# Accumulators of the last convolution tile in PSUM, a running sum issued behind a K eviction, and two V tiles ahead of the memory attention

## The chip, the core and the metric

The kernel runs on one core of one Trainium2 chip. What is measured is the device time of one launch, in microseconds (us), as the median of several runs. TensorE (PE) multiplies, VectorE (DVE), ScalarE (ACT) and GpSimd (POOL) do the elementwise work, SyncE (SP) issues most transfers. SBUF is the core's large on-chip memory, PSUM the small one in which TensorE accumulates; it has banks of 512 fp32 columns by 128 partitions.

## The reference

A decoder trunk of two layers over 1024 tokens of width 1024, all in fp32. Layer A projects the normalised input to the 2 x 768 columns of a gated convolution and to the queries of four memory heads. Then one projection gives K, V and the forget gates of twelve heads, and layer B attends with them. Each layer ends in an output projection, a residual sum and a feed-forward block with a convolution of its own.

```python
def conformer_conv(u, b_glu, w_dw, b_dw, ln_g, ln_b):
    u = u + b_glu
    a, gate = jnp.split(u, 2, axis=-1)
    v = a * jax.nn.sigmoid(gate)
    v = causal_dwconv(v, w_dw, b_dw)          # 31 taps, each channel by itself
    v = layernorm(v, ln_g, ln_b)
    return jax.nn.silu(v)
...
        logits = jnp.einsum("bqhd,bkhd->bhqk", qb, kb).astype(jnp.float32) * scale
        logits = logits + cum_logf[:, :, q0:kend, None] - cum_logf[:, :, None, :kend]
        ...
        p = jax.nn.softmax(logits, axis=-1).astype(vb.dtype)
        outs.append(jnp.einsum("bhqk,bkhd->bqhd", p, vb))
```

`cum_logf` is the running sum of the logarithms of the forget gates over the tokens. The memory attention is an ordinary softmax attention of four heads over 256 memory tokens; it is computed beside the convolution in layer A and beside the forgetting attention in layer B.

## The kernel before

Channels lie on the 128 partitions, tokens along the free dimension, in two halves `hf` of 512 (HS). Every fp32 operand is split into a high and a low part (`..h`, `..l`, line 81 and 82), and one product is three matmuls, high by high, high by low, low by high (`mm3`, lines 108 to 110). A scheduler sets each engine's order from the order of the code, from priorities (`later`) and from a model of costs; `issue_after` keeps an instruction behind a named one.

PSUM is handed out by tags: `c0` to `c3` are one bank each, `b2` is two pairs of banks, and a tile with a tag waits until the tile before it under that tag has been read for the last time. Long projections are cut into small steps, the "fill". `set_fill` takes the list of steps, `drain_fill(n)` issues the next n at once, and `mark` issues some of them behind a matmul of the attention code, so that TensorE has other work while a softmax runs.

**The convolution of layer A** (`conv_steps`) has six channel tiles of 128. The 31 taps of a tile are shared out. The first `NPE` run on TensorE as products with diagonal matrices `dg` into the PSUM tile `cpe`. The next `NPOOL` are products on ScalarE (`ct`, L874) that GpSimd adds up in `yp` (L875). The rest run on VectorE. For tiles 0 to 4 VectorE adds its taps into `cpe` (L918, 1024 columns) and then `yp` and `cpe` into `v` (L919). The last tile has 8 taps on TensorE, 13 for ScalarE and GpSimd and 10 on VectorE; VectorE works there half by half on an accumulator of its own, `nca`, in SBUF: one product (L886) and nine multiply-adds (L888) for each half, and one addition into `yp` (L889). L914 then adds `yp` and `cpe` into `v`, half by half. `ua` is the value projection that yields `v` (L958), `vl` the low part of `v`, `ug` the gate.

Beside this runs `mem_attention`: scores `ms` (L259, L260), their maximum `nm` (L262), exponentials `amp` on ScalarE (L265), the reciprocal `r` of their sum (L267), the normalisation of `amp` on GpSimd (L230), a transpose `mt` on TensorE (L276), its two parts `mth` on ScalarE (L278) and `mtl` on VectorE (L279), and the product with V into `mo` (L280, L281). Behind it come partial output projections `om`, which VectorE adds to the residual `x` (L1004), and the LayerNorm of the convolution (`lnorm`): for each half six matmuls `mean` with a constant column, one for each channel tile (L1014), into a PSUM tile under tag `c0` or `c1`; then differences (L1019), squares `nlsq` (L1021) and their sums `lst` on TensorE (L1023).

**Layer B** begins with the memory queries `pq` of both halves, under tags `c0` and `c1`; VectorE scales them (L240) by the row `rb`, which for each half needs a column sum `st` (L133), a reciprocal `rs` (L142) and a broadcast matmul `bc` (L123), and takes their low parts (`bmq`, L247). The fill there is the V projection: 24 matmuls `vps` (L1122) for each of eight token tiles in three passes, each tile evicted on ScalarE and VectorE (`vo` L1129, and the gates `fl` L1131).

After V comes the K and Q projection of head pairs t (`kq_steps`): 8 steps for each half of K, then 8 for each half of Q, each step three matmuls into `pq`. From t = 1 on both halves use the same bank, `c0`. The eviction of K is L1181, that of Q is L1183. The first 32 steps (t = 0) are drained ahead of the gates' logarithms. These are transposed to 12 x 1024 (`lft`, copies L1211), and VectorE forms their running sum `bcum` in one scan (L1215). Its two parts `bch` (L1218) and `bcl` (L1219) and their negatives (L1224, L1225) go to memory (`d_c`) and from there into the extra rows of q and k that bring the bias into the scores `fs` (L1260, L1261). 20 more steps (`AHEAD`) of the fill follow before the first scores. The weights `wk_raw` and `wq_raw` are scaled on GpSimd when they arrive (L99); `ps` are the softmax weights, normalised on GpSimd as well (L230).

Of the kernel before, what the change touches and what calls it, by code (L numbers as in the profile page):

```python
# [8 lines left out]
F32 = mybir.dt.float32  # L9
# [3 lines left out]
ALU = mybir.AluOpType  # L13
AX = mybir.AxisListType

P = 128
S = 1024
HS = 512
# [12 lines left out]
VP = 260  # L31
# [20 lines left out]
class Trunk:  # L52
# [668 lines left out]
    def layer_a(self):  # L721
        nc, tc = self.nc, self.tc
# [130 lines left out]
        def conv_steps(t):  # L853

            v = vts[t]
            w = lambda j: self.vec("w_dwa", t * CW + j)
            ne = self.NPE[t]
            np_ = ne + self.NPOOL[t]
            last = t == CT - 1
            d = {}  # L860


            def start():
                d["vh"] = pb.tile([P, CW - 1 + S], F32R, tag="vh", name="vh")
                d["vl"] = pb.tile([P, CW - 1 + S], F32R, tag="vl", name="vl")
                self.split(d["vh"], d["vl"], v, lo_eng=nc.vector)
                with self.later(self.LATER):
                    y = d["y"] = pb.tile([P, 2, HS], F32, tag="yp", name="yp", bufs=2)
                    for hf in range(2):
                        nc.scalar.activation(y[:, hf], v[:, hf * HS + ne:hf * HS + ne + HS], AF.Identity,  # L870
                                             bias=self.vec("b_dwa", t), scale=w(ne))
                        for j in range(ne + 1, np_):
                            c = pb.tile([P, HS], F32, tag="ct", name="ct", bufs=2)
                            nc.scalar.activation(c, v[:, hf * HS + j:hf * HS + j + HS], AF.Copy, scale=w(j))  # L874
                            nc.gpsimd.tensor_tensor(y[:, hf], y[:, hf], c, op=ALU.add)  # L875
                if last:

                    with self.later(self.LATER):
                        d["a"] = []
                        for hf in range(2):  # L880
                            a = self.nt("ca")
                            d["a"].append(a)
                            for j in range(np_, CW):
                                vj = v[:, hf * HS + j:hf * HS + j + HS]
                                if j == np_:
                                    nc.vector.tensor_scalar(a, vj, w(j), None, op0=ALU.mult)  # L886
                                else:
                                    nc.vector.scalar_tensor_tensor(a, vj, w(j), a, op0=ALU.mult, op1=ALU.add)  # L888
                            nc.vector.tensor_tensor(y[:, hf], y[:, hf], a, op=ALU.add)  # L889


            def tap(j, hfs):
                if j == 0 and hfs[0] == 0:
                    d["pe"] = self.ps.tile([P, 2, HS], F32, tag="b2", name="cpe")
                    d["g"] = {}
                if j not in d["g"]:
                    g = d["g"][j] = pb.tile([P, 2, P], F32R, tag="dg", name="dg", bufs=8)
                    for i, wt in enumerate((wth, wtl)):
                        nc.scalar.activation(g[:, i], self.ident, AF.Copy,
                                             scale=wt[:, t * CW + j:t * CW + j + 1].bitcast(F32))  # L900
                g = d["g"][j]
                for hf in hfs:
                    sl = slice(hf * HS + j, hf * HS + j + HS)
                    self.mm3(d["pe"][:, hf], [(g[:, 0], g[:, 1], d["vh"][:, sl], d["vl"][:, sl])],
                             start=j == 0, stop=j == ne - 1)
                if j == ne - 1:
                    rest(hfs)


            def rest(hfs):  # L910
                with self.later(self.LATER):
                    if last:
                        for hf in hfs:
                            nc.vector.tensor_tensor(v[:, hf * HS:(hf + 1) * HS], d["y"][:, hf], d["pe"][:, hf], op=ALU.add)  # L914
                        return
                    a = d["pe"].rearrange("p a b -> p (a b)")
                    for j in range(np_, CW):
                        nc.vector.scalar_tensor_tensor(a, v[:, j:j + S], w(j), a, op0=ALU.mult, op1=ALU.add)  # L918
                    nc.vector.tensor_tensor(v[:, :S], d["y"].rearrange("p a b -> p (a b)"), a, op=ALU.add)  # L919
            d["start"] = start  # L920
            d["taps"] = [lambda j=j, h=h: tap(j, h) for h in (((0,), (1,)) if last else ((0, 1),)) for j in range(ne)]
            return d
# [122 lines left out]
    def layer_b(self):  # L1045
        nc, tc = self.nc, self.tc
# [3 lines left out]
        def pth(dt, nm):  # L1050
            return pc.tile([P, HS], dt, tag="pt", name=nm, bufs=6)

        wqm = self.load_w(self.wib[CT], [KD, P], gains=self.vec("g_mix1", 0, KD), name="wqm0")
        xh, xl, rb, cols = self.normed("b", None, tmp1=lambda nm, w: pth(F32, nm))
# [51 lines left out]
        def v_steps(pc_):  # L1106

            d = {}

            def step(i):  # L1110
                t, kk = i // 4, i % 4
                hf, ti = t // 4, t % 4
                if i == 0:
                    load_v(pc_ + 1)
                if kk == 0:
                    d["ps"] = self.ps.tile([P, VP], F32, tag=f"c{t % 2}", name="vps")
                ps = d["ps"]
                tsl = slice(ti * P, (ti + 1) * P)
                for k in (2 * kk, 2 * kk + 1):
                    wh, wl = wv[pc_][k // 4]  # L1120
                    for j, (a, w) in enumerate(((xh, wh), (xl, wh), (xh, wl))):
                        nc.tensor.matmul(ps, lhsT=a[hf][k][:, tsl], rhs=w[:, k % 4], start=k == 0 and j == 0,  # L1122
                                         stop=k == KD - 1 and j == 2)
                if kk == 3:
                    r = cols[hf][:, ti:ti + 1]
                    vo = vp.tile([P, 4, P], F32R, tag="vo", name="vo", bufs=3)
                    pv_ = ps[:, :MEM].rearrange("p (h d) -> p h d", h=4)
                    nc.scalar.activation(vo[:, :, :DH], pv_, AF.Copy, scale=r)
                    nc.vector.scalar_tensor_tensor(vo[:, :, DH:], pv_, r, vo[:, :, :DH].bitcast(F32),  # L1129
                                                   op0=ALU.mult, op1=ALU.subtract)  # L1130
                    nc.vector.scalar_tensor_tensor(fl[:, t, 4 * pc_:4 * pc_ + 4], ps[:, MEM:], r,  # L1131
                                                   self.bf[:, 4 * pc_:4 * pc_ + 4], op0=ALU.mult, op1=ALU.add)
                    nc.sync.dma_start(self.d_v[pc_, :, :, t], vo.bitcast(F32))
            return [lambda i=i: step(i) for i in range(32)]
# [12 lines left out]
        for e in range(2):  # L1147
            d = {n: pb.tile([P, S], F32R, tag=f"{n}{e}", name=f"{n}{e}") for n in ("q1", "q2", "k1", "k2")}
# [16 lines left out]
        def kq_steps(t):  # L1165

            d = kqv[t] = {}

            def step(i):
                n, hf, k = ("k", "q")[i // 16], i // 8 % 2, i % 8  # L1170
                sl = slice(hf * HS, (hf + 1) * HS)
                if i % 16 == 0:
                    load(2 * t + (n == "q") + 1)
                    d["w" + n] = ws.pop((t, n))
                    d[n] = unit([P, S], F32, n + "c")
                if k == 0:
                    d["u"] = self.ps.tile([P, HS], F32, tag="c1" if t == 0 and hf else "c0", name="pq")
                proj_half(d["w" + n], d["u"], hf, [k])
                if k == KD - 1:
                    if n == "k":  # L1180
                        nc.vector.tensor_tensor(d[n][:, sl], d["u"], rb[:, sl], op=ALU.mult)  # L1181
                    else:
                        nc.vector.scalar_tensor_tensor(d[n][:, sl], d["u"], SCALE, rb[:, sl],  # L1183
                                                       op0=ALU.mult, op1=ALU.mult)
            return [lambda i=i: step(i) for i in range(32)]
# [20 lines left out]
        lf = unit([NFOX, S], F32, "lf")  # L1206
# [5 lines left out]
        on = unit([NFOX, S], F32, "on")  # L1212
        nc.gpsimd.memset(on, 1.0)
        cum = unit([NFOX, S], F32, "cum")
        nc.vector.tensor_tensor_scan(cum, on, lf, 0.0, op0=ALU.mult, op1=ALU.add)  # L1215
        ch = unit([NFOX, S], F32R, "ch")
        cl = unit([NFOX, S], F32R, "cl")
        nc.scalar.copy(ch, cum)  # L1218
# [86 lines left out]
                    nc.tensor.matmul(po, lhsT=vs[:, j], rhs=pl[:, u], start=False, stop=j == 2 * I + 1)  # L1305
            self.fold_rows(o, po, e, self.nt("fr", 2 * P))

        self.drain_fill(self.AHEAD)
        vss = {(0, 0): prep(0, 0), (0, 1): prep(0, 1)}
        its = [(t, e, I) for t in range(CT) for e in range(2) for I in range(4)]  # L1310
        pend = []
# [268 lines left out]
```

## Time and profile before

| | |
|---|---|
| median of 3 runs | 2335.38 us (2333.52 to 2335.58) |
| the profiled execution | 2334.59 us, of which the span of the trace is 2332.8 us |
| busy: PE, DVE, ACT, POOL | 2256.2, 1460.0, 1075.5, 1333.7 us |
| instructions | 29689 |

The span runs from the first to the last instruction in the trace. A row of a timeline gives start, duration, engine, line, operation, `out<-in` with the names of tiles, the shape, and in brackets the idle time of the engine ahead of it with what ended it. "x8" means that so many records in a row are shown as one. The lines are those of the kernel before.

### The profile page before, as it was taken

To read this page: it belongs to the slowest core of one execution; us is meant where nothing else is said; L and a number is where in the kernel's file an instruction comes from. 1 tells how busy PE (TensorE), PEld (TensorE's weight loads), DVE (VectorE), ACT (ScalarE), POOL (GpSimd) and SP (SyncE) were. 2 spreads that over 40 slices of the span, in tenths; PEclk is the share of its full clock that TensorE was granted. 3 is DMA by queue.
4 is the path that set the end of the run, shared out by engine and by line. 5 is a ranking of instruction groups with operands and counts; after the bars stand their busy time and mean duration, and the time that the engine had idled before them with its cause. 6 is when DMAs were issued, how large, how long until landed. Compare 5 with 4: busy or idle time off the path is not lost.

```text
span 2332.8 us, 29689 instructions
## 1 busy us (share of the span) xinstructions
PE 2256.2 (97%) x10970; PEld 1865.7 (80%) x10970; DVE 1460.0 (63%) x1995; ACT 1075.5 (46%) x1864; POOL 1333.7 (57%) x1003
## 2 busy tenths in 40 slices
PE   6999889999999999999998999999999999999998
PEld 6777668878788878888897888788878888778887
DVE  7479787676666664325656777876776666645225
ACT  6776746443434343223542666755444343442212
POOL 3676844666868676453323443614577777766533
PEclk8999989999999999999999999999999999999999
DMA  6100023222222235332332222433222222245322
GB/s 242 37 28 28 29 73 117 72 81 82 82 76 88 78 108 188 106 109 95 123 105 81 71 77 68 124 110 127 67 86 75 81 75 88 79 136 175 112 68 73
DMA packets 85282, 216.74 MB, mean 93 GB/s; under 512 B 9009, under 2 KB 29233, under 8 KB 85137
## 3 DMA queue, kind: packets, MB, share of 16 engines
q1 hardware_dynamic: 84992, 214.52, 28.8%
q8 instruction: 86, 1.41, 0.3%
q14 instruction: 60, 0.48, 0.1%
q10 hardware_dynamic: 144, 0.32, 0.0%
HBM read 156.94 MB, written 51.58 MB: 89 GB/s over the span
## 4 chain that ended last, share of the span: by engine, by line
PE 46%; DVE 3%; POOL 1%; ACT 1%; issue 1%; DMA 0%; DVEq 0%; ACTq 0%; POOLq 0%
PE uY L345 8%; PE uX L345 5%; PE uV L345 5%; PE dn L109 3%; PE dn L108 3%; PE dn L110 3%; PE vps L1122 3%; PE pq L108 2%; PE pq L110 2%; PE pq L109 2%; PE op L108 1%; PE op L109 1%; PE op L110 1%; PE fo L1305 1%; PE fs L1260 1%; PE fo L1304 1%
## 5 line engine op out<-in xcount | busy, mean ns | idle before, releaser
L345 PE MATMUL uY<-fT,fwh 128*128 128x512 f32 x1056 | 331.4, 395 | 4.7 <-DVE fuv L546 3.2
L109 PE MATMUL dn<-gl,wd_hi 128*128 128x512 f32 (+1 forms) x752 | 284.6, 379 | 1.2 <-POOL gl L82 1.2
L108 PE MATMUL dn<-gh,wd_hi 128*128 128x512 f32 (+1 forms) x752 | 280.3, 377 | 0.0
L662 DVE TENSOR_TENSOR fx<-fx,dn 128x512 f32<-128x512 f32 (+1 forms) x176 | 110.9, 636 | 268.8 <-PE dn L110 268.5
L110 PE MATMUL dn<-gh,wd_lo 128*128 128x512 f32 (+1 forms) x752 | 278.9, 375 | 0.0
L345 PEld LDWEIGHTS uY<-fT,fwh 128*128 128x128 f32 x1056 | 196.3, 188 | 55.3 <-DVE fuv L546 9.8
L345 PE MATMUL uX<-fB,fwh 128*128 128x512 f32 x704 | 220.0, 393 | 2.0 <-ACT fuv L521 1.9
L345 PE MATMUL uY<-fT,fwl 128*128 128x512 f32 x528 | 206.6, 391 | 0.0
L82 POOL TENSOR_TENSOR fwl<-wa,fwh 128x512 fp32r<-128x512 f32 x88 | 117.1, 1331 | 137.6 <-ACT fwh L81 137.5
L82 POOL TENSOR_TENSOR wd_lo<-wd_raw,wd_hi 128x1024 fp32r<-128x1024 f32 x44 | 107.9, 2458 | 137.8 <-ACT wd_hi L81 129.0
L108 PEld LDWEIGHTS dn<-gh,wd_hi 128*128 128x128 f32 x752 | 141.2, 188 | 28.3
L109 PEld LDWEIGHTS dn<-gl,wd_hi 128*128 128x128 f32 x752 | 141.3, 188 | 27.0 <-POOL gl L82 2.0
L110 PEld LDWEIGHTS dn<-gh,wd_lo 128*128 128x128 f32 x752 | 141.0, 188 | 27.1
L345 PEld LDWEIGHTS uX<-fB,fwh 128*128 128x128 f32 x704 | 131.6, 188 | 33.3 <-ACT fuv L521 2.8
L82 POOL TENSOR_TENSOR fwl<-wb,fwh 128x512 fp32r<-128x512 f32 x88 | 121.9, 1387 | 63.1 <-ACT fwh L81 60.8
L875 POOL TENSOR_TENSOR yp<-yp,ct 128x512 f32<-128x512 f32 x100 | 135.7, 1359 | 27.6 <-ACT ct L874 22.7
L82 POOL TENSOR_TENSOR gl<-g,gh 128x512 fp32r<-128x512 f32 x88 | 117.5, 1357 | 47.1 <-ACT gh L81 47.1
L345 PE MATMUL uX<-fB,fwl 128*128 128x512 f32 x352 | 137.3, 392 | 0.0
L82 POOL TENSOR_TENSOR fwl<-fs,fwh 128x512 fp32r<-128x512 f32 x88 | 117.8, 1340 | 20.1 <-ACT fwh L81 20.1
L81 ACT CAST fwh<-wa 128x512 fp32r<-128x512 f32 x88 | 54.2, 618 | 140.7 <-PE uY L345 108.3
L81 ACT CAST wd_hi<-wd_raw 128x1024 fp32r<-128x1024 f32 x44 | 45.6, 1050 | 157.6 <-issue 82.2
L345 PEld LDWEIGHTS uY<-fT,fwl 128*128 128x128 f32 x528 | 99.2, 188 | 22.3
(398 smaller groups left out, 6285.4 us busy)
## 6 DMA issues: line engine op xcount, KB each, us to landing
wb<-in_wup SPq DMA_DIRECT2D x44, 512.0 KB
wa<-in_wup SPq DMA_DIRECT2D x44, 512.0 KB
d_g<-fsg SPq DMA_DIRECT2D x44, 512.0 KB
wd_raw<-in_wdn SPq DMA_DIRECT2D x44, 512.0 KB
g<-d_g SPq DMA_DIRECT2D x44, 512.0 KB
d_x<-x SPq DMA_DIRECT2D x32, 256.0 KB
nxs<-d_x SPq DMA_DIRECT2D x32, 256.0 KB
wia_raw<-in_wia SPq DMA_DIRECT2D x14, 512.0 KB
```

What stands on the lines that cost most here:

```text
L81: nc.scalar.copy(hi, src)
L82: (lo_eng or nc.gpsimd).tensor_tensor(lo, src, hi.bitcast(F32), op=ALU.subtract)
L108: nc.tensor.matmul(out, lhsT=ah, rhs=bh, start=start and i == 0, stop=False)
L109: nc.tensor.matmul(out, lhsT=ah, rhs=bl, start=False, stop=False)
L110: nc.tensor.matmul(out, lhsT=al, rhs=bh, start=False, stop=stop and i == n - 1)
L345: mm = nc.tensor.matmul(out, lhsT=w[:, k], rhs=h[k], start=start and k == 0 and j == 0, stop=k == n - 1 and j == 2, skip_group_check=True)
L662: return nc.vector.tensor_tensor(self.x[m][:, sl], self.x[m][:, sl], ps, op=ALU.add)
L875: nc.gpsimd.tensor_tensor(y[:, hf], y[:, hf], c, op=ALU.add)
L1122: nc.tensor.matmul(ps, lhsT=a[hf][k][:, tsl], rhs=w[:, k % 4], start=k == 0 and j == 0, stop=k == KD - 1 and j == 2)
L1260: mm = nc.tensor.matmul(o, lhsT=d["q1"][:, qs], rhs=d["k1"][:, ksl], start=True, stop=False)
L1304: nc.tensor.matmul(po, lhsT=vs[:, j], rhs=ph[:, u], start=j == 0, stop=False)
L1305: nc.tensor.matmul(po, lhsT=vs[:, j], rhs=pl[:, u], start=False, stop=j == 2 * I + 1)
```

## The change

Three places are edited. `last_k` is a new attribute and holds the last K eviction that was issued.

```diff
                         for hf in range(2):
-                            a = self.nt("ca")
+                            a = self.ps.tile([P, HS], F32, tag=f"c{hf}", name="ca")
                             d["a"].append(a)
...
                 if kk == 0:
-                    d["ps"] = self.ps.tile([P, VP], F32, tag=f"c{t % 2}", name="vps")
+                    d["ps"] = self.ps.tile([P, VP], F32, tag=f"c{t % 2 + 2 * (t < 2 and pc_ == 0)}", name="vps")
...
                     if n == "k":
-                        nc.vector.tensor_tensor(d[n][:, sl], d["u"], rb[:, sl], op=ALU.mult)
+                        self.last_k = nc.vector.tensor_tensor(d[n][:, sl], d["u"], rb[:, sl], op=ALU.mult)
...
         cum = unit([NFOX, S], F32, "cum")
-        nc.vector.tensor_tensor_scan(cum, on, lf, 0.0, op0=ALU.mult, op1=ALU.add)
+
+        self.drain_fill(8)
+        with self.issue_after(self.last_k.ins):
+            nc.vector.tensor_tensor_scan(cum, on, lf, 0.0, op0=ALU.mult, op1=ALU.add)
...
-        self.drain_fill(self.AHEAD)
+        self.drain_fill(self.AHEAD - 8)
```

**A.** The accumulator of the last convolution tile, half `hf`, is a PSUM tile `ca` under tag `c{hf}`, no longer an SBUF tile. The `mean` tile of that half has the same tag, so it comes into being after L889 has read `ca`. On TensorE, four of the six `mean` matmuls of the first half stood ahead of `mt`, with their order now (behind the last `cpe` of the first half, ahead of those of the second):

```order
 L109 MATMUL cpe<-vl,dg 128x512
 L110 MATMUL cpe<-vh,dg 128x512
-L1014 MATMUL mean<-v_686,inv_conv 128x512
-L1014 MATMUL mean<-v_688,inv_conv 128x512
-L1014 MATMUL mean<-v_690,inv_conv 128x512
-L1014 MATMUL mean<-v_692,inv_conv 128x512
 L276 MATMUL mt<-ident,amp 128x128 x4
 L108 MATMUL cpe<-vh,dg 128x512
```
```order
 L109 MATMUL cpe<-vl,dg 128x512
 L110 MATMUL cpe<-vh,dg 128x512
+L1014 MATMUL mean<-v_686,inv_conv 128x512
+L1014 MATMUL mean<-v_688,inv_conv 128x512
+L1014 MATMUL mean<-v_690,inv_conv 128x512
+L1014 MATMUL mean<-v_692,inv_conv 128x512
 L108 MATMUL cpe<-vh,dg 128x512
 L109 MATMUL cpe<-vl,dg 128x512
```

The four of the second half, which stood after L958, now stand with the other two of that half behind 12 + 6 `om` matmuls. On ScalarE the order at the same `mt` was, with `v_694` the fifth and `v_696` the last tile,

```order
L874 ACTIVATE ct<-v_694,vecs 128x512
L899 ACTIVATE dg<-ident,wth 128x128
L899 ACTIVATE dg<-ident,wtl 128x128
L899 ACTIVATE dg<-ident,wth 128x128
L899 ACTIVATE dg<-ident,wtl 128x128
L899 ACTIVATE dg<-ident,wth 128x128
L899 ACTIVATE dg<-ident,wtl 128x128
L874 ACTIVATE ct<-v_696,vecs 128x512 x3
L278 CAST mth<-mt 128x512
L874 ACTIVATE ct<-v_696,vecs 128x512
```

and is now

```order
L874 ACTIVATE ct<-v_694,vecs 128x512
L899 ACTIVATE dg<-ident,wth 128x128
L899 ACTIVATE dg<-ident,wtl 128x128
L874 ACTIVATE ct<-v_696,vecs 128x512
L899 ACTIVATE dg<-ident,wth 128x128
L899 ACTIVATE dg<-ident,wtl 128x128
L899 ACTIVATE dg<-ident,wth 128x128
L899 ACTIVATE dg<-ident,wtl 128x128
L278 CAST mth<-mt 128x512
L874 ACTIVATE ct<-v_696,vecs 128x512
```

so that two `ct` of the last tile moved behind `mth`. GpSimd does one more `yp` addition before the normalisation of `amp`.

**B.** In the first V pass, token tiles 0 and 1 take the tags `c2` and `c3` in place of `c0` and `c1`. On TensorE at the start of the memory attention of layer B the rows were

```order
L123 MATMUL bc<-ident,rs 128x128 x4
L133 MATMUL st<-ones_69,sq 128x1 x4
L123 MATMUL bc<-ident,rs 128x128 x4
L259 MATMUL ms<-bks_8602,bmq 128x256
L260 MATMUL ms<-bks_8603,bmq 128x256
```

and now begin

```order
L123 MATMUL bc<-ident,rs 128x128 x4
L133 MATMUL st<-ones_69,sq 128x1 x4
L1122 MATMUL vps<-wv_hi,bh_8453 128x260
L1122 MATMUL vps<-wv_hi,bl_8469 128x260
L1122 MATMUL vps<-wv_lo,bh_8453 128x260
L1122 MATMUL vps<-wv_hi,bh_8454 128x260
```

All 24 matmuls of V tile 0 moved from behind eight `ms` matmuls to the place between `st` and the second `bc`. Tile 1 and 18 matmuls of tile 2 then follow the `ms`, and later ones have less of them between. The evictions of tile 0 (`vo`, `fl`) stand ahead of the second half's `rb` copy on ScalarE and of its scaling L240 on VectorE.

**C.** Eight of the 20 steps that stood behind the scan are drained ahead of it: the first half of K of head pair 1. The scan is kept behind that half's eviction. On VectorE the rows were

```order
L82 TENSOR_TENSOR wk_lo<-wk_raw,wk_hi 128x1024
L1211 COPY blf<-lft 12x512
L1215 SCALAR_TENSOR_TENSOR bcum<-bon,blf 12x1024
L1219 TENSOR_TENSOR bcl<-bcum,bch 12x1024
L1181 TENSOR_TENSOR bkc<-pq,rb 128x512 x2
```

and are now, with three added to the numbers of lines from the scan on,

```order
L82 TENSOR_TENSOR wk_lo<-wk_raw,wk_hi 128x1024
L1211 COPY blf<-lft 12x512
L1181 TENSOR_TENSOR bkc<-pq,rb 128x512
L1218 SCALAR_TENSOR_TENSOR bcum<-bon,blf 12x1024
L1222 TENSOR_TENSOR bcl<-bcum,bch 12x1024
L1181 TENSOR_TENSOR bkc<-pq,rb 128x512
```

The first K eviction moved ahead of the scan, the second stayed behind `bcl`. On TensorE the bias matmuls `fs` (L1261) moved behind 18 matmuls of the Q projection, and on GpSimd the scaling of `wq_raw` (L99) moved ahead of the first normalisation of `ps` (L230).

## The prediction

> **What bounds the kernel now.** I read the page's first part, then the waits of TensorE, then the windows round each wait, and last the timeline of each engine there.
>
> ```profile
> PE 2256.2 (97%) x10970; PEld 1865.7 (80%) x10970; DVE 1460.0 (63%) x1995; ACT 1075.5 (46%) x1864; POOL 1333.7 (57%) x1003
> ```
>
> TensorE is busy in 97% of the 2332.8 us span; 76.6 us of idle time are all that reordering could win. The waits say where (engine, line and tile, what it waited for, us, times, longest):
>
> ```profile
> PE pq L108 <- DVE bkc L1181: 6.9, 2, 6.4
> PE cpe L108 <- DVE v L914: 6.3, 1, 6.3
> PE bc L123 <- DVE rs L142: 4.6, 2, 3.6
> PE mo L280 <- ACT mth L278: 2.8, 2, 2.2
> ```
>
> Three places hold these: the last convolution tile (A, `cpe` and `mo`), the start of the memory attention of layer B (B, `bc`), the second K projection (C, `pq`). The windows (PE, PEld, DVE, ACT, POOL busy, then granted clock, DMA share, GB/s) show what lies between them:
>
> ```profile
> 262.00:332.00 70.00, 57.04 (x221) 40.61 (x220) 63.85 (x69) 36.69 (x73) 52.78 (x42) 0.90 0.21 72
> 1108.00:1132.00 24.00, 19.40 (x113) 16.80 (x112) 16.97 (x22) 14.47 (x30) 12.84 (x10) 0.93 0.45 148
> 1250.00:1282.00 32.00, 24.79 (x113) 19.25 (x112) 19.03 (x24) 11.08 (x18) 12.81 (x8) 0.89 0.22 57
> 340.00:1100.00 760.00, 755.98 (x3332) 616.63 (x3332) 444.00 (x522) 298.61 (x441) 467.76 (x331) 1.00 0.29 96
> 1290.00:2200.00 910.00, 900.67 (x4441) 740.99 (x4440) 599.61 (x880) 432.24 (x755) 534.61 (x393) 1.00 0.31 96
> ```
>
> Around A TensorE has 57.04 of 70 us and a clock of 0.90, and VectorE with 63.85 is the fullest engine. Between the places TensorE is busy 99% at full clock. So work there only waits for TensorE: what is won in A should reach B, and what is won in B and C the end. I therefore add the three terms.
>
> **A, the accumulators in PSUM.** Two things change: the price of 22 VectorE instructions, and the order round them. First the price (groups by shape; busy us, mean ns, idle before):
>
> ```profile
> L918 DVE SCALAR_TENSOR_TENSOR cpe<-v,vecs,cpe 128x1024 f32<-128x1024 f32 x85 | 108.8, 1282 | 5.1 <-PE cpe L110 3.8
> L888 DVE SCALAR_TENSOR_TENSOR nca<-v,vecs,nca 128x512 f32<-128x512 f32 x18 | 19.6, 1091 | 0.2
> L886 DVE TENSOR_SCALAR nca<-v,vecs 128x512 f32<-128x512 f32 x2 | 2.9, 1456 | 0.1
> L889 DVE TENSOR_TENSOR yp<-yp,nca 128x512 f32<-128x512 f32 x2 | 2.7, 1370 | 0.0
> L914 DVE TENSOR_TENSOR v<-yp,cpe 128x512 f32<-128x512 f32 x2 | 1.3, 673 | 0.0
> ```
>
> No row shows an accumulator `ca` in PSUM with 512 columns. The nearest is L918, the same operation with `cpe` in PSUM: 1282 ns for 1024 columns, so about 640 for 512, and L914, one operand in PSUM at 512, with 673. The other end is no gain, 1091 as in SBUF. I take 670: 18 x 0.42 + 2 x 0.79 + 2 x 0.70 = 10.5 us of VectorE time, some 6 of it in the second half's 11 instructions, where VectorE never rests. [...]
>
> Now the order. `mean` of each half uses the bank that `ca` now holds, so four early `mean` matmuls per half move behind L889; and ScalarE's `mth` copy stands behind one `ct` of the last tile, where it stood behind three. ScalarE and VectorE, start and duration, with the idle time before:
>
> ```profile
> 275.01 0.72 ACT L874 ACTIVATE ct<-v,vecs 128x512 f32<-128x512 f32 x1 [2.77 <-POOL yp L875]
> ...
> 278.57 0.56 ACT L278 CAST mth<-mt 128x512 fp32r<-128x512 f32 x1
> ```
> ```profile
> 279.17 0.69 DVE L279 TENSOR_TENSOR mtl<-mt,mth 128x512 fp32r<-128x512 f32 x1 [3.64 <-ACT mth L278]
> ...
> 286.72 0.75 DVE L958 SCALAR_TENSOR_TENSOR v<-ua,vecs,sg 128x512 f32<-128x512 f32 x1
> ...
> 305.92 0.67 DVE L914 TENSOR_TENSOR v<-yp,cpe 128x512 f32<-128x512 f32 x1
> ...
> 323.95 0.67 DVE L914 TENSOR_TENSOR v<-yp,cpe 128x512 f32<-128x512 f32 x1
> ```
> ```profile
> 269.70 3.60 POOL L230 TENSOR_SCALAR amp<-amp,r 128x256 f32<-128x256 f32 x4 [1.52 <-DVE r L267]
> ...
> 308.63 2.27 POOL L230 TENSOR_SCALAR amp<-amp,r 128x256 f32<-128x256 f32 x4 [0.78 <-ACT ct L874]
> ...
> 317.75 2.63 POOL L875 TENSOR_TENSOR yp<-yp,ct 128x512 f32<-128x512 f32 x2 [0.72 <-ACT ct L874]
> ```
> ```profile
> 270.17 3.59 PE L1014 MATMUL mean<-v,inv_conv 128*128 128x512 f32 x8
> ...
> 287.52 5.40 PE L1014 MATMUL mean<-v,inv_conv 128*128 128x512 f32 x8 [2.09 <-DVE v L958]
> ...
> 329.26 2.51 PE L1023 MATMUL lst<-ones,nlsq 128*128 128x1 f32 x22
> ```
>
> Before, `mth` sat until 278.57 behind `ct` copies that waited for GpSimd, VectorE idled 3.64 us for it, and from 279.17 on the whole stretch was a VectorE chain. Now the normalisation of `amp` on GpSimd (3.60 beside SBUF accumulators, 2.27 elsewhere) ends near 271.3, one `yp` add ahead of it included, since VectorE's cheaper accumulators release `r` sooner; `mt` follows, and `mth` at 271.7. VectorE owes four accumulator steps by then, so its chain starts some 6.2 us earlier, and L958 comes at about 279.8. Behind it the cheaper instructions take out another 2 us up to the first L914 (297 against 305.92) and 3 more up to the second (312.4 against 323.95), where GpSimd's last `yp` add, now near 311, is late next. Then comes the price: ahead of the second half's statistics TensorE must then do all six `mean` matmuls of that half. Four cost 3.59, so six cost 5.4, where before the last two were left (each `mean` matmul leaves two records, so x8 is four of them). With the transfer and six `om` matmuls between, the first `lst` falls at 320.5 to 321.2 against 329.26: 8 us. The four of the first half cost nothing; they land in the 6.3 us that TensorE waits for L914, and if that cover is gone their 3.6 us are the loss. The row at 287.52 shows 5.40 us for what took 3.59 at 270.17, so the clock falls even after waits of 2 us; for new waits of that kind I take off 1. A: -7, ends -9.5 (no slow clock) and +2 (GpSimd's chain keeps its time, so that L914 stays near 323 and six `mean` matmuls follow it).
>
> **B, two V tiles on free banks.** Tiles 0 and 1 use banks that no memory query holds. Their matmuls' order changes, nothing is added.
>
> ```profile
> 1115.24 1.05 PE L123 MATMUL bc<-ident,rs 128*128 128x128 f32 x8
> 1116.13 0.95 PE L133 MATMUL st<-ones,sq 128*128 128x1 f32 x8
> 1120.69 1.68 PE L123 MATMUL bc<-ident,rs 128*128 128x128 f32 x8 [3.62 <-DVE rs L142]
> ...
> 1124.51 0.41 PE L1122 MATMUL vps<-wv_hi,bh 128*128 128x260 f32 x1
> ...
> 1127.39 0.28 PE L1122 MATMUL vps<-wv_lo,bh 128*128 128x260 f32 x1
> ```
>
> TensorE idles 3.62 us for `rs`, and 24 `vps` matmuls, 1124.51 to 1127.5, are 3.0 us of work that now stands in that gap: their inputs were there before 1116. `bc` shows 1.68 after the idle and 1.05 before it, so the clock adds 0.6, and about as much in the eight `ms`. Upper end 3.0 + 1.2 = 4.2. Against it: tile 0's evictions now stand ahead of the second query half on ScalarE and VectorE, and the later stretch of `ms` and `mt` has less filler. I take off 1.2: B = -3, ends -4.2 and -1 (the softmax waits come back where the filler was).
>
> **C, the running sum behind the K eviction.** Both halves of a K tile share one bank, so the second half's matmuls wait for the eviction L1181 of the first, which stood behind the scan on VectorE. PE, then VectorE, then GpSimd:
>
> ```profile
> 1264.08 0.79 PE L108 MATMUL pq<-bh,wk_hi 128*128 128x512 f32 x1 [6.42 <-DVE bkc L1181]
> ...
> 1268.02 0.40 PE L108 MATMUL pq<-bh,wk_hi 128*128 128x512 f32 x1
> ...
> 1271.23 0.39 PE L110 MATMUL pq<-bh,wk_lo 128*128 128x512 f32 x1
> ...
> 1272.49 0.47 PE L108 MATMUL pq<-bh,wq_hi 128*128 128x512 f32 x1 [0.44 <-DVE bkc L1181]
> ```
> ```profile
> 1256.98 3.68 DVE L1215 TENSOR_TENSOR_SCAN bcum<-bon,blf 12x1024 f32<-12x1024 f32 x1
> ...
> 1261.76 1.66 DVE L1219 TENSOR_TENSOR bcl<-bcum,bch 12x1024 fp32r<-12x1024 f32 x1 [1.11 <-ACT bch L1218]
> ```
> ```profile
> 1277.75 1.90 POOL L99 TENSOR_TENSOR wq_raw<-wq_raw,vecs 128x1024 f32<-128x1024 f32 x1 [2.78 <-DMA wq_raw<-in_wib]
> ```
>
> TensorE resumes about 0.7 us after its last matmul, so 5.7 of the 6.42 go; nine matmuls from 1264.08 to 1268.02 are 0.44 apart, the 14 after them 0.23, so 1.9 more goes with the slow clock. That is 7.6. Given back: the scan, `bch` and `bcl` now lie ahead of the second eviction, which ends near 1265.4, 1.6 after its matmuls (before 0.44): 1.2. The sums' transfers to and from memory start 1.2 later; 18 `wq` matmuls, 4.1 us at 0.23, now ahead of the bias matmuls cover them. GpSimd's scaling of `wq_raw` (1.90) moves ahead of the first softmax normalisation, so the first transposes of `ps` and the third block's scores come late by an estimated 1.5. C = -5, ends -6.5 and -2.5.
>
> The sum is -15 on the profiled execution's 2334.59, which is 0.8 below the median of 2335.38: 2319.6 and 2320.4; I say 2320.
>
> **The rivals.** One: A gives nothing, because GpSimd's 24 `yp` adds set the tail and all six `mean` matmuls follow them. For it speaks that POOL is the second fullest engine there (52.78 of 70); against it that the adds wait for `ct` and that the contended 3.60 should fall. A = +1, sum -7: 2327.5. The same holds within 2 us if the accumulators keep SBUF's price (A near -1). Two: A works, but B and C only move their waits into the softmax chains behind them (-1 and -2.5): 2335 - 10.5 = 2324.5. Three, no change: all three gains are taken back by a late transfer in the stretches between, for which only the DMA share of 0.29 to 0.31 there could speak, and it is low; 2335. Four, slower, by one mechanism: VectorE's accumulators in PSUM cost more than in SBUF. It decides from the point where 22 instructions eat the 15 us and 5 beyond, 0.9 us more each than 0.67, about 1.6 us. At twice L888's 1091 it would be 22 x 1.51 = 33, less 15: 2353. L918 reads and writes PSUM at 1282 for twice the columns, so I hold this for unlikely.
>
> **How the numbers follow.** The forecast as it stands has 0.55, one 0.2, two 0.1, three 0.1, four and whatever else ends slower 0.05. The ends together are -9.5 - 4.2 - 6.5 = -20 (2315) and +2 - 1 - 2.5 = -1.5 (2333.5). The range runs from 2312, 3 below the former for a slow clock of which I undervalue the end, to 2331, which takes in one and two. Within 0.2%, about 4.7 us, this kernel's measurement can't tell a change from none, so faster means below 2330.7: the forecast, one and two, 0.85; same 0.1; slower 0.05.
>
> **What would show it.** In A: `mth` near 272, the accumulators at 0.64 to 0.70, no wait of 6 us for L914, `lst` some 8 us earlier, and 5.4 us of `mean` after the second L914. In B: `vps` between `st` and the second `bc`, whose wait falls under 1 us. In C: the first K wait under 1 us, the second eviction's over 1. Wrong it is if the accumulators stay above 1 us, if `lst` does not move, or if the stretch from 340 to 1100 grows by what A won.

## The result, and the profile after

The changed kernel takes 2316.99 us (median of 4, 2316.4 to 2317.25) against 2334.45 for the kernel before in the same comparison: a ratio of 0.9925, interval 0.9908 to 0.9942, 17.5 us faster. Its profiled span is 2315.1 us, 17.7 less. The first part of the page, and TensorE's waits (us in total, times, longest):

```profile
PE 2250.8 (97%) x10970; PEld 1861.1 (80%) x10970; DVE 1452.4 (63%) x1995; ACT 1074.7 (46%) x1864; POOL 1332.5 (58%) x1003
```
```profile
PE cpe L108 <- ACT vh L81: 2.6, 1, 2.6
PE uY L345 <- DVE fug L525: 2.5, 2, 1.7
PE cpe L109 <- DVE vl L82: 2.2, 1, 2.2
...
PE pq L108 <- DVE bkc L1181: 1.4, 2, 0.9
PE mo L280 <- ACT mth L278: 1.4, 2, 0.7
...
PE bc L123 <- DVE rs L142: 0.9, 1, 0.9
PE fs L1263 <- ACT ps L1274: 0.9, 2, 0.6
```

TensorE is busy 5.4 us less on the same 10970 matmuls, at a mean granted clock of 0.992 where before had 0.988, and idle 64.3 instead of 76.6 us, 12.3 less. So the 76.6 us of idle time were not all that reordering could win: 5.4 of the 17.7 us came out of busy time. The waits of 6.4, 6.3 and 3.6 us are gone; two of 2.6 and 2.2, on the parts of the last tile's `v`, are new.

**A.** VectorE's accumulator groups, and its timeline at the start of the last tile (its first L958) and at the four instructions shown for before:

```profile
L888 DVE SCALAR_TENSOR_TENSOR ca<-v,vecs,ca 128x512 f32<-128x512 f32 x18 | 13.5, 748 | 0.2
L886 DVE TENSOR_SCALAR ca<-v,vecs 128x512 f32<-128x512 f32 x2 | 1.5, 750 | 0.0
L889 DVE TENSOR_TENSOR yp<-yp,ca 128x512 f32<-128x512 f32 x2 | 1.4, 680 | 0.3 <-POOL yp L875 0.3
```
```profile
264.18 0.75 DVE L958 SCALAR_TENSOR_TENSOR v<-ua,vecs,sg 128x512 f32<-128x512 f32 x1 [1.60 <-PE ua L110]
...
272.80 0.69 DVE L279 TENSOR_TENSOR mtl<-mt,mth 128x512 fp32r<-128x512 f32 x1 [0.29 <-ACT mth L278]
...
279.85 0.75 DVE L958 SCALAR_TENSOR_TENSOR v<-ua,vecs,sg 128x512 f32<-128x512 f32 x1
...
296.37 0.67 DVE L914 TENSOR_TENSOR v<-yp,cpe 128x512 f32<-128x512 f32 x1
...
312.11 0.69 DVE L914 TENSOR_TENSOR v<-yp,cpe 128x512 f32<-128x512 f32 x1
```

`mtl` comes 6.4 us earlier, the second L958 6.9, the first L914 9.6 and the second 11.8. The start of the chain shows in the transpose `mt` and its copy `mth`, first in before (the copy, at 278.57, is shown in the prediction), then now:

```profile
273.61 0.60 PE L276 MATMUL mt<-ident,amp 128*128 128x128 f32 x4
```
```profile
271.40 0.60 PE L276 MATMUL mt<-ident,amp 128*128 128x128 f32 x4
```
```profile
272.20 0.57 ACT L278 CAST mth<-mt 128x512 fp32r<-128x512 f32 x1
```

`mt` itself gains 2.2 us, and the copy now follows it at once, where before it came 4.4 us after the end of `mt`: two thirds of the earlier start are the copy's new place on ScalarE. On TensorE, `mean` stands where the order said:

```profile
286.65 0.80 PE L109 MATMUL cpe<-vl,dg 128*128 128x512 f32 x1 [2.17 <-DVE vl L82]
...
295.30 3.60 PE L1014 MATMUL mean<-v,inv_conv 128*128 128x512 f32 x8
...
313.79 5.31 PE L1014 MATMUL mean<-v,inv_conv 128*128 128x512 f32 x12
...
320.33 1.84 PE L1023 MATMUL lst<-ones,nlsq 128*128 128x1 f32 x16
```

The first `lst` is 8.9 us earlier. About 0.9 of that is lost by layer B: TensorE's busy time between 340 and 1100 falls from 755.98 to what this row gives, and in this stretch the longest wait of `uY` for `fug` is 1.7 us (in the waits above) where it was 0.8.

```profile
340.00:1100.00 760.00, 755.08 (x3316) 615.37 (x3316) 443.83 (x518) 298.56 (x442) 471.79 (x334) 1.00 0.29 98
```

**B and C.** TensorE, and then VectorE round the scan:

```profile
1107.30 1.05 PE L123 MATMUL bc<-ident,rs 128*128 128x128 f32 x8
...
1110.12 0.39 PE L1122 MATMUL vps<-wv_hi,bh 128*128 128x260 f32 x1 [0.35 <-ACT sd L140]
...
1113.10 1.05 PE L123 MATMUL bc<-ident,rs 128*128 128x128 f32 x8
...
1246.14 0.50 PE L108 MATMUL pq<-bh,wk_hi 128*128 128x512 f32 x1 [0.55 <-DVE bkc L1181]
...
1252.74 0.47 PE L108 MATMUL pq<-bh,wq_hi 128*128 128x512 f32 x1 [0.87 <-DVE bkc L1181]
...
1258.15 0.44 PE L1263 MATMUL fs<-k,q 128*128 128x384 f32 x1 [0.62 <-ACT ps L1274]
```
```profile
1245.39 0.69 DVE L1181 TENSOR_TENSOR bkc<-pq,rb 128x512 f32<-128x512 f32 x1 [0.59 <-PE pq L110]
1246.00 2.59 DVE L1218 TENSOR_TENSOR_SCAN bcum<-bon,blf 12x1024 f32<-12x1024 f32 x1
...
1251.91 0.69 DVE L1181 TENSOR_TENSOR bkc<-pq,rb 128x512 f32<-128x512 f32 x1 [0.54 <-PE pq L110]
```

The first `bc` of the memory attention is at 1107.30 instead of 1115.24, so A brings 7.9 us there, counted from the start of the span. The last tile, however, began 1.2 us later in this execution (264.18) than in before (262.95), and A has no part in that. TensorE met the same wait of 2.69 us at 248 in both, and behind it the granted clock stayed at 1.00 in before and fell to 0.79 here, as it also did in the run of C alone, none of whose edits is in layer A (0.81). The rows, before and then after (busy PE, PEld, DVE, ACT, POOL, then clock, DMA share, GB/s):

```profile
248.00:256.00 8.00, 7.31 (x34) 6.07 (x35) 5.53 (x7) 6.44 (x9) 6.24 (x5) 1.00 0.05 17
```
```profile
248.00:256.00 8.00, 7.64 (x29) 6.28 (x30) 4.51 (x5) 5.32 (x9) 5.56 (x5) 0.79 0.01 2
```

From the start of the last tile to the first `bc`, A brings 9.2 us against before, and 8.5 against C alone (263.74 to 1115.33). The K wait began at 1264.08 - 6.42 = 1257.66 and begins now at 1246.14 - 0.55 = 1245.59, 12.1 us earlier, so B adds 4.1. The rest to the span's 17.7 is C's, 5.6. In B the second `bc` follows the `vps` without a wait and at 1.05 us, where it took 1.68. In C the scan takes 2.59 us where it took 3.68; here and in C alone (2.60) it runs beside the last 0.5 us of a GpSimd sum into `q`, in before beside the last 1.5. That this is the cause is not shown.

### The profile page after: what moved, and what is told of

Its sections match the earlier page's. It is cut to its first block, busy times and chain, and to the rows that moved or that the text cites. A ratio compares the mean times of both kernels' runs of the same rounds, so it can differ in the third digit from the quotient of the medians.

```text
span 2315.1 us, 29688 instructions
## 1 busy us (share of the span) xinstructions
PE 2250.8 (97%) x10970; PEld 1861.1 (80%) x10970; DVE 1452.4 (63%) x1995; ACT 1074.7 (46%) x1864; POOL 1332.5 (58%) x1003
## 4 chain that ended last, share of the span: by engine, by line
PE 88%; DVE 6%; ACT 3%; issue 2%; POOL 1%; DMA 1%; DVEq 0%; ACTq 0%; POOLq 0%
PE uY L345 15%; PE uX L345 10%; PE uV L345 10%; PE dn L109 7%; PE dn L108 7%; PE dn L110 7%; PE vps L1122 3%; PE op L108 2%; PE op L109 2%; PE op L110 2%; PE pq L108 2%; PE pq L110 2%; PE pq L109 2%; PE fo L1308 1%; PE fo L1307 1%
## 5 line engine op out<-in xcount | busy, mean ns | idle before, releaser
L108 PEld LDWEIGHTS dn<-gh,wd_hi 128*128 128x128 f32 x752 | 141.1, 188 | 28.2
L110 PEld LDWEIGHTS dn<-gh,wd_lo 128*128 128x128 f32 x752 | 141.1, 188 | 27.1
L82 POOL TENSOR_TENSOR fwl<-fs,fwh 128x512 fp32r<-128x512 f32 x88 | 117.9, 1340 | 19.6 <-ACT fwh L81 19.6
```

Source lines behind the costliest of these rows:

```text
L82: (lo_eng or nc.gpsimd).tensor_tensor(lo, src, hi.bitcast(F32), op=ALU.subtract)
L108: nc.tensor.matmul(out, lhsT=ah, rhs=bh, start=start and i == 0, stop=False)
L110: nc.tensor.matmul(out, lhsT=al, rhs=bh, start=False, stop=stop and i == n - 1)
```

## The experiments

**Are the three gains independent?** Theory: each is a wait of its own, and the sum is the change. Rival: they overlap or need each other. One run for each edit alone, that is, the diff of the change cut to its first line, to its second, and to the three of C.

> Only the accumulators in PSUM. If the three edits are independent and each gain is carried to the end by the stretches where TensorE is 99% busy, this is 7.5 us faster than before (2327), with 0.75 us for each accumulator step and the first lst near 320. If the gains overlap (a stretch behind A takes part of any gain), it is more than 9 faster alone and the three singles add to more than 17.5; if they need each other, less than 5.

> Only the two V tiles on free banks. Independent edits: 4.1 us faster (the shift that the trace of the full change gains between 1109 and 1180), the wait for rs under 1 us. The rival, that B's gain comes from A having moved the weights' transfers: 1 us or less.

> Only eight K steps and their eviction ahead of the scan. Independent edits: 5.8 us faster, the wait of 6.4 us for the K eviction under 1 us. The rival (the time comes back in the softmax chain behind it): 3 or less.

| edit alone | us | ratio to before (interval) | us gained |
|---|---|---|---|
| A | 2324.6 | 0.9959 (0.9947 to 0.9972) | 9.7 |
| B | 2331.3 | 0.9986 (0.9977 to 0.9995) | 3.0 |
| C | 2328.47 | 0.9976 (0.9967 to 0.9985) | 5.8 |

They add up to 18.5 us against 17.5 for the change. The theory's three numbers (7.5, 4.1, 5.8) all lie in the intervals, and nothing speaks for edits that need each other: A alone gave 9.7 where that rival had less than 5. Full independence is not shown: both signs that I had set for an overlap came, 9.7 past 9 and 18.5 past 17.5, though well inside the intervals. The traces, one of each, point to a small overlap. In the run of A alone TensorE's longest wait for `rs` is 2.5 us, in before 3.6; in the run of B alone it is 1.4, where I had expected less than 1 (A alone, then B alone; times, longest in the last two columns):

```profile
PE bc L123 <- DVE rs L142: 3.4, 2, 2.5
```
```profile
PE bc L123 <- DVE rs L142: 1.4, 1, 1.4
```

From the first `bc` to the start of the K wait it is 142.4 us in before, 141.7 in C alone, where nothing is changed up to there, 141.1 in A alone, and 138.3 in the full change. So A alone seems to hold already 0.6 to 1.3 us of the 4.1 that I put down to B; why, no run shows. The other expectations came: with A alone the step takes 748 ns and the first `lst` is at 320.62; with C alone the longest wait for the K eviction is 0.9 us.

**Which half of A matters, the start or the cheap steps?** Theory: most of A is the earlier start, which hangs on the first half's accumulator. Rival: the second half, where VectorE never idles.

```diff
-a = self.nt("ca")
+a = self.ps.tile([P, HS], F32, tag=f"c{hf}", name="ca") if hf == 0 else self.nt("ca")   # and hf == 1
```

> Of A only the first half's accumulator in PSUM, the second in SBUF. Theory: the first half brings the earlier start (the softmax copy mth near 272, since it stands behind one ct and GpSimd's normalisation is short beside PSUM accumulators), 6 us at L958, and the second half's four mean matmuls are not moved to the tail; the second half's steps stay above 0.9 us beside GpSimd. 4 to 7 us faster than before. Rival: only the price of the second half counts, since VectorE idles 3.6 us in the first: 0 to 2 faster.

> Of A only the second half's accumulator in PSUM. Theory: mth stays near 278.5, VectorE's chain starts at 279 as before and gains only some 5 us up to the second L914 by cheaper steps; the last mean matmuls take part of it back: 2 to 4 us faster than before. Rival (the price of the second half is all): 6 to 9 faster.

The first half alone gives 2328.27 us, ratio 0.9973 (0.9964 to 0.9982), 6.1 us; the second half alone 2332.85, ratio 0.9992 (0.9983 to 1.0), 1.5 us, a little less than the theory's 2 to 4, with an interval that reaches to no gain. The rival, 6 to 9 us from the second half, falls. The halves add up to 7.6 us where A alone gave 9.7, a difference inside the intervals. L958, the step groups and TensorE's longest new wait, first half alone:

```profile
280.09 0.75 DVE L958 SCALAR_TENSOR_TENSOR v<-ua,vecs,sg 128x512 f32<-128x512 f32 x1
```
```profile
L888 DVE SCALAR_TENSOR_TENSOR nca<-v,vecs,nca 128x512 f32<-128x512 f32 x9 | 9.3, 1037 | 0.0
L888 DVE SCALAR_TENSOR_TENSOR ca<-v,vecs,ca 128x512 f32<-128x512 f32 x9 | 6.8, 754 | 0.2
```
```profile
PE mean L1014 <- DVE yp L889: 5.8, 1, 5.8
```

and L958 in the second half alone:

```profile
286.64 0.75 DVE L958 SCALAR_TENSOR_TENSOR v<-ua,vecs,sg 128x512 f32<-128x512 f32 x1
```

With the first half in PSUM, L958 stands at 280.09, almost where the full change has it; with the second, at 286.64, where it was before. In one kernel, nine steps in SBUF take 1037 ns each and nine in PSUM 754. TensorE's 5.8 us there are the first half's `mean` matmuls, which now wait for L889. The run does not part the first half's cheaper steps from the new order on ScalarE; both come with that accumulator.

**Why are steps in SBUF slow?** Theory: they wait for GpSimd. Rival: accumulating in SBUF is slow by itself.

```diff
                             nc.scalar.activation(c, v[:, hf * HS + j:hf * HS + j + HS], AF.Copy, scale=w(j))
-                            nc.gpsimd.tensor_tensor(y[:, hf], y[:, hf], c, op=ALU.add)
+                            if not last:
+                                nc.gpsimd.tensor_tensor(y[:, hf], y[:, hf], c, op=ALU.add)
```

> The kernel before, leaving out GpSimd's 24 additions of ct into yp in the last convolution tile (their taps are missing from the sum). Theory: an SBUF accumulator step is slow only beside a GpSimd instruction that uses SBUF, so L888 falls from a mean of 1.09 us to about 0.75, the price in PSUM, except where other GpSimd work runs. Rival: SBUF accumulation is slow by itself: L888 stays above 1.

VectorE's timeline, six steps of the first half and then the second half (lines are one higher than in before, L889 is the step), and the GpSimd work that meets a step of the second:

```profile
271.79 5.97 DVE L889 SCALAR_TENSOR_TENSOR nca<-v,vecs,nca 128x512 f32<-128x512 f32 x6
...
290.10 0.52 DVE L887 TENSOR_SCALAR nca<-v,vecs 128x512 f32<-128x512 f32 x1
...
300.63 0.74 DVE L889 SCALAR_TENSOR_TENSOR nca<-v,vecs,nca 128x512 f32<-128x512 f32 x1
...
303.07 0.74 DVE L889 SCALAR_TENSOR_TENSOR nca<-v,vecs,nca 128x512 f32<-128x512 f32 x1
...
304.99 0.94 DVE L889 SCALAR_TENSOR_TENSOR nca<-v,vecs,nca 128x512 f32<-128x512 f32 x1
...
307.05 0.74 DVE L889 SCALAR_TENSOR_TENSOR nca<-v,vecs,nca 128x512 f32<-128x512 f32 x1
```
```profile
304.00 2.28 POOL L230 TENSOR_SCALAR amp<-amp,r 128x256 f32<-128x256 f32 x4 [10.04 <-DVE r L267]
```

Steps in SBUF take 0.74 us while GpSimd rests, as in PSUM, and the one step that meets `amp` takes 0.94. In the first half, where adds of the tile before and `amp` still run, they keep to 1 us (5.97 for six). The theory holds: the price is GpSimd's, and PSUM only takes the accumulator out of its way. This kernel was timed only once, so its time is not compared.

**Can the displaced `mean` matmuls be had back?** The full change left waits of 2.6 and 2.2 us just where four `mean` matmuls had stood. If the last accumulator step writes into SBUF, the bank comes free there:

```diff
                                 else:
-                                    nc.vector.scalar_tensor_tensor(a, vj, w(j), a, op0=ALU.mult, op1=ALU.add)
+                                    a, a0 = (a if j < CW - 1 else self.nt("ca")), a
+                                    nc.vector.scalar_tensor_tensor(a, vj, w(j), a0, op0=ALU.mult, op1=ALU.add)
```

> The full change, and the last accumulator step of each half writes to an SBUF tile, so that the bank comes free at that step and not after the addition into yp. Theory: in the full change TensorE idles 2.6 and 2.2 us (waits for vh and vl near 283 and 287) since the four mean matmuls that stood there had to move behind L889; given the bank back they stand there again, and those of the second half no longer stand at the tail: 3 to 5 us faster than the full change, 2312 to 2314. Rival: the tail is set by GpSimd's yp adds and the second L914 near 312, and the mean matmuls only fill time that is idle later: within 1.5 us of the full change.

It takes 2317.19 us, ratio to before 0.9927 (0.9914 to 0.9939), the same as the full change. My theory fell. The `mean` matmuls did go back into the gap, but TensorE then met other waits:

```profile
291.89 0.39 PE L259 MATMUL ms<-aks,amq 128*128 128x256 f32 x1 [2.16 <-ACT amp L265]
...
298.26 0.79 PE L108 MATMUL cpe<-vh,dg 128*128 128x512 f32 x1 [4.73 <-DVE v L915]
```

(L915 is L914 there.) The four matmuls had been hiding the wait of `cpe` for the first L914, at 296.4 in the full change and 297.5 here. VectorE's chain did not get earlier by it; `mth` now waits for a `mt` that stands behind `mean` matmuls, and the second L914 comes 3.3 us later than in the full change (312.11):

```profile
311.78 0.69 DVE L279 TENSOR_TENSOR mtl<-mt,mth 128x512 fp32r<-128x512 f32 x1 [1.73 <-ACT mth L278]
...
315.38 0.68 DVE L915 TENSOR_TENSOR v<-yp,cpe 128x512 f32<-128x512 f32 x1
```

The first `lst` is earlier all the same, at 315.39 for 320.33, and the first `bc` of layer B is not (1107.80 for 1107.30): where the order changes, an early `lst` is no measure of the gain.

I then tried to take that wait away, by issuing the taps of both halves of `cpe` together, with the last step in SBUF as above:

```diff
-            d["taps"] = [lambda j=j, h=h: tap(j, h) for h in (((0,), (1,)) if last else ((0, 1),)) for j in range(ne)]
+            d["taps"] = [lambda j=j, h=h: tap(j, h) for h in ((0, 1),) for j in range(ne)]
```

> As the run in which the last accumulator step writes to SBUF, and the taps of both halves of the last tile are issued together on TensorE, so that no cpe matmul of the second half waits for L914 of the first (4.7 us there). Theory: TensorE then gets ahead of VectorE's chain and 2 to 4 us are won against the full change. Rival: VectorE's chain with 17 L918 steps and GpSimd's yp adds set the time of both L914, whatever TensorE does before: within 1.5 us of the full change.

2321.12 us, ratio 0.9943 (0.9927 to 0.9958): no gain, and some 4 us behind the full change, though the two intervals overlap. So neither my theory nor its rival, which had it within 1.5 us of the full change, came true. The `cpe` work is done early, and TensorE waits 6.4 us for the softmax instead:

```profile
304.68 1.85 PE L276 MATMUL mt<-ident,amp 128*128 128x128 f32 x4 [6.39 <-POOL amp L230]
```

In both runs TensorE was handed work earlier, and its wait moved to the next product of ScalarE, VectorE or GpSimd. Why the last one is slower than the full change, and not only as fast, is not shown. No version that was run beats the change.

## Why the prediction was right

The forecast was 2320 us in a range of 2312 to 2331, and 2317.0 was measured. All three terms had the right mechanism and were somewhat small: A -7 (7.9 to 9.2 in the trace, 9.7 alone), B -3 (4.1 and 3.0), C -5 (5.6 and 5.8). Of the signs named beforehand two failed: the accumulators' 0.64 to 0.70 us, and over 1 us for the wait behind the second eviction.

**A, the price.** 670 ns taken from L914 was too low: the step takes 748, with a spread of only 739 to 756, and the lone product L886 750 where 670 was taken for it as well. Half of L918's 1282 ns was too low as well: 1282 - 748 leaves 534 ns for 512 columns, and so, by estimate, some 214 that do not shrink with the width. The 22 instructions cost 16.4 us for 25.2 before (19.6 + 2.9 + 2.7), a saving of 8.8, not 10.5. PSUM did not make the step dearer: it takes 0.74 us in SBUF beside a quiet GpSimd (the steps at 300.63 and 303.07 in the run without GpSimd's adds) and 748 ns in PSUM.

**A, the order.** The chain came out as worked: L958 279.8 by forecast and 279.85 measured, the first L914 297 and 296.4, the second 312.4 and 312.1, `lst` 320.5 to 321.2 and 320.3. That the times agree so closely is partly luck: the last tile began 1.2 us later than in before, so counted from there the chain won more than forecast, 8.1 us for 6.9 at L958. GpSimd's last add is the late one, as forecast (the 0.3 at L889), and six `mean` matmuls of 5.3 us follow. What I took off for a slow clock did come: after the waits of 2.6 and 2.2 us the `cpe` matmuls ran slowly, 0.43 us apart from 287.24 to 292.36 and 0.23 from 292.74 on, but that lay under VectorE's chain. One detail was wrong: the first half's `mean` matmuls do not land in a wait of 6.3 us for L914, which had gone with the rest. They take its place, and as the last-step run shows, moving them away brings the wait back and wins nothing.

**B.** The 1.2 us set against it hardly came. In the attention that follows, up to 1185, TensorE's timeline has one wait:

```profile
1123.58 0.50 PE L280 MATMUL mo<-mth,bvs 128*128 128x512 f32 x1 [0.69 <-ACT mth L278]
```

In before one of 0.60 stood in the same stretch. The trace of B alone bears out the 4.1: its first `bc` stands at 1113.46, 1.8 us earlier than in before, and its K wait begins at 1258.16 - 6.42 = 1251.74, 5.9 earlier.

```profile
1258.16 0.80 PE L108 MATMUL pq<-bh,wk_hi 128*128 128x512 f32 x1 [6.42 <-DVE bkc L1181]
```

The median of 3.0 has 4.1 in its interval.

**C.** The second eviction was charged with 1.2 us, a wait of 1.6 for 0.44 before. The wait is 0.87, and it is not the scan's: VectorE was done with the sums and idled 0.54 us for the last K matmul, which in the full change is this one:

```profile
1251.48 0.39 PE L110 MATMUL pq<-bh,wk_lo 128*128 128x512 f32 x1
```

From it to the first Q matmul it is 1.26 us (1252.74), and in before it was 1.26 as well (1271.23 to 1272.49), but with bias matmuls in between that now stand elsewhere. The shorter scan kept it so: with the 3.68 us of before, the second eviction would by estimate have come some 0.5 us later. Of the 1.5 at the first scores, 0.62 came for the third block.

In rival one GpSimd was called the second fullest engine of its window; by the row it is the third, with 52.78 us behind VectorE's 63.85 and TensorE's 57.04. The rivals: GpSimd's chain did not keep its time (one), B and C kept their gains (two), the long stretch took back 0.9 us (a trace of three), and 748 ns is far from the 1.6 us at which four would decide.

## What to carry to other kernels

Before pricing an instruction from its mean, look at what else uses the memory at that moment: here a spread of 737 to 1759 ns within one group was the sign, and an operand moved to PSUM brought the group to its floor (748 ns on average) and shortened GpSimd's work too (the normalisation of `amp` from 3.60 to 1.85 us). When a buffer is moved, look at what had the place before: its work goes elsewhere, and whether that costs depends on which engine's chain sets the pace there. Where the next matmuls reuse the bank, the eviction belongs ahead of a long instruction that nobody waits for yet: here that was worth 5.6 us. And before two traces are compared at one place, look whether they entered the stretch at the same time: here they were 1.2 us apart for a reason outside the change.

## What of the hardware was not expected

The contention is mutual. VectorE's accumulator step took 1091 ns on average in SBUF before and takes 748 in PSUM. And GpSimd's normalisation of `amp` at this place took 3.60 us before; with the accumulators in PSUM it takes 1.85, less than the 2.27 that I took for its undisturbed time:

```profile
269.58 1.85 POOL L230 TENSOR_SCALAR amp<-amp,r 128x256 f32<-128x256 f32 x4
```

How the two engines come to slow each other, no run shows.

The one instruction that a run shows slower with PSUM is the plain product (L886 of before): 0.52 us from SBUF to SBUF in the run without GpSimd's adds (at 290.10), 0.75 into PSUM in the changed kernel. Why, no run shows. With two such instructions in the kernel it does not count.

TensorE's clock fell after two waits of 2.6 and 2.2 us with five matmuls between: the granted clock in that window (busy PE, PEld, DVE, ACT, POOL, then clock) is 0.72.

```profile
282.00:300.00 18.00, 15.00 (x46) 10.74 (x47) 17.91 (x21) 11.56 (x23) 17.37 (x14) 0.72 0.56 196
```

A wait of this size does not always do it: behind the wait of 2.69 us at 248, the clock was 1.00 in before and 0.79 in the changed kernel. What decides it, no run shows.
